# The same instructions at other addresses: SBUF tiles of the large matmuls moved to multiples of 2 KB

## The chip, the cores and the metric

The kernel runs on one core of a Trainium2 chip. The metric is the device time of one execution in microseconds (us); lower is better. SBUF is the on-chip memory, 128 partitions wide; in this text an address is a byte offset within a partition, and a tile of 1024 float32 columns takes 4,096 bytes of it. PSUM is the memory that TensorE writes its results to.

## The reference, cut to what matters

The reference runs a sequence of 256 positions of width 1024 through four layers and then through one further block, all in float32. Layers 0 and 3 use banded attention with 16 heads and a relative bias, layer 1 a gated linear attention, layer 2 a differential attention; each is followed by a layer norm, a SwiGLU feed-forward part of hidden width 2816 and a second layer norm. The last block is a SwiGLU part, a mixer (indexed sparse attention beside a gated short convolution), a cross-attention to 256 memory positions, and another SwiGLU part, with RMS norms between them.

```
h = layer_norm(DN_ALPHA * h + mixer_i(h), ln1_g[i], ln1_b[i])
h = layer_norm(DN_ALPHA * h + (silu(h @ Wg) * (h @ Wu)) @ Wd, ln2_g[i], ln2_b[i])      # i = 0..3
...
h = h + 0.5 * rms_norm(swiglu(rms_norm(h)))        # and the mixer, cross-attention, a second swiglu
```

Nearly all arithmetic is in the products of the 256 x 1024 activations with weight matrices: some 340 MB of weights are read once.

## The kernel before, in words

**Split products.** A float32 product is made out of three float32r products. Every weight piece of 128 x 1024 arrives by DMA in a tile `raw` (5 buffers); ScalarE writes its rounded part `wh` (L274, 10 buffers) and VectorE the rest `wl` (L275, 10 buffers). Activations are held transposed and split in the same way: `sth0`, `stl0`, `sth1`, `stl1` (128 x 8 x 128, one buffer each, for the two halves of the sequence) for products that go in from width 1024, and `gth0`, `gtl0`, `gth1`, `gtl1` (128 x 4 x 128, two buffers each) for products that go out to width 1024. The function `mm3` then issues three matmuls: the weights are the moving operand, 512 columns at a time, and a 128 x 128 slice of the activations is the stationary operand, loaded anew for each matmul.

```
for o, w in zip(outs, whs): nc.tensor.matmul(o, xh, w, start=first, stop=False)   # L286
for o, w in zip(outs, wls): nc.tensor.matmul(o, xh, w, start=False, stop=False)   # L288
for o, w in zip(outs, whs): nc.tensor.matmul(o, xl, w, start=False, stop=last)    # L290
```

`lin` uses `st` slices and one PSUM bank named `lin`; slice number kt goes from 0 to 7, and the three matmuls of one kt follow one another. `lin_out` uses `gt` slices and two banks named `acc`, alternating between the halves of the output. There are 5,040 matmuls of 512 columns in `lin` and 2,256 in `lin_out`, and 48 of 200 columns. One product is the other way round: for the gate of layer 1 (L705 to L707) the moving operand is a 128-column slice of `sth` or `stl`, and the stationary one has 16 columns.

**Other tiles.** `t2` (4 buffers of 128 x 512), `q2`, `v2`, `b4`, `p4`, `pt4`, `bc`, `k4` (4,128 bytes, 2 buffers) and `sm` (20 buffers of 64 bytes) hold what lies between: keys, queries, probabilities, biases, gains, row sums. `ident` is the identity for transposes on TensorE (L332, L606); `mhalf` and `ones` are small constants.

**Order of work.** The two halves of the sequence are two generators that are stepped in turn, so that each weight piece serves both. The whole list of instructions is then put into an order for each engine by a planner (`plan_order`, `play`, `order_issue`): it simulates engines, buffers and DMA with fixed costs and due times, and its order is written into the program as dependences. The planner looks at each tile's name, at the region of the tile that an instruction touches, at the tag and at the number of buffers; it does not look at addresses.

**Addresses.** A pool gives each tag its buffers side by side, in the order in which tags are first asked for. In the compiled kernel before, four constants of the framework lie ahead of the pool, which begins at 16,512. The offsets from a multiple of 2,048 are: 128 for `h0`, `h1`, `raw`, `wh`, `wl` and `ident`; 704 for `sth0`, `stl0`, `t2`, `sth1`, `stl1`; 704 and 736 for `k4`; 768 for `q2`, `b4`, `p4`; 0 for `pt4`, `v2`, `gth0`, `gtl0`, `gth1`, `gtl1` and `bc`, which come right after `sm`.

Of the kernel before, what the change touches and what calls it, by code (L numbers as in the profile page):

```python
# [208 lines left out]
class Net:  # L209
# [154 lines left out]
    def setup(self):  # L364
        nc, A = self.nc, self.A
        self.cache = {}
        self.toep = {}
        self.h = [self.t(f"h{tt}", [128, D], 1) for tt in range(2)]
        for c in range(2):
            nc.sync.dma_start(self.h[0][:, 512 * c:512 * c + 512], A["x"][0, 0:128, 512 * c:512 * c + 512])  # L370
            self.emit_splits(1 + c)
        self.ident = self.t("ident", [128, 128], 1)
        make_identity(nc, self.ident)
        self.mhalf = self.t("mhalf", [128, 8], 1)
        nc.gpsimd.memset(self.mhalf, -0.5)
        self.ones = self.t("ones", [128, 1], 1)
        nc.gpsimd.memset(self.ones, 1.0)

    def setup1(self):
# [1046 lines left out]
```

## Time and profile before

| | |
|---|---|
| median of 3 runs | 1947.97 us (1946.9 to 1948.11) |
| the profiled execution | 1947.88 us, of which the span from first to last instruction is 1946.1 us |
| TensorE matmuls | 1918.8 us busy, 99% of the span |
| VectorE, ScalarE, GpSimd | 60%, 48%, 2% |
| mean granted clock of TensorE | 0.998 |
| DMA | 345.59 MB, mean 178 GB/s |

Matmuls overlap one another, and their ends are modelled, so the sum of their durations is more than the span; the pace is read from their starts. PE is TensorE's matmul, PEld its load of the stationary operand.

### The profile page before, as it was taken

How to read it: one execution, taken by the hardware profiler on the slowest of the kernel's cores; microseconds unless marked ns; L12 is line 12 of the kernel's file. 1: busy time of each engine (PE TensorE's matmuls, PEld its weight loads, DVE VectorE, ACT ScalarE, POOL GpSimd, SP SyncE). 2: the span in 40 equal slices, each digit the busy share in tenths (PEclk: the TensorE clock that was granted, in tenths of full speed). 3: DMA queues.
4: the chain of work that ended last, by engine and by line, in shares of the span. 5: the costliest groups of instructions: out<-in, count | busy, mean ns of one | idle time of the engine just before them, and what ended most of it. 6: DMA issues, size and time to landing. Idle time of an engine off the chain costs nothing.

```text
span 1946.1 us, 23881 instructions
## 1 busy us (share of the span) xinstructions
PE 1918.8 (99%) x8998; PEld 1535.1 (79%) x8998; DVE 1168.2 (60%) x1687; ACT 926.6 (48%) x1332; POOL 48.5 (2%) x71
## 2 busy tenths in 40 slices
PE   8999999999999999999999999999999999999998
PEld 6888887777888777888778888878887788788886
DVE  5565547666456767555756645664567957565454
ACT  5545444544444554444554544444444545545442
POOL 0000000000000000000000000000001000000000
PEclk9999999999999999999999999999999999999999
DMA  9536555646555545555544655465555456536562
GB/s 300 166 133 224 183 183 158 210 150 226 181 183 168 175 149 176 189 184 179 186 149 148 217 182 183 153 222 183 185 169 171 139 176 205 162 121 205 180 187 66
DMA packets 103293, 345.59 MB, mean 178 GB/s; under 512 B 13369, under 2 KB 20473, under 8 KB 103178
## 3 DMA queue, kind: packets, MB, share of 16 engines
q1 hardware_dynamic: 103178, 344.07, 54.3%
q8 instruction: 70, 1.15, 0.2%
q14 instruction: 45, 0.37, 0.1%
HBM read 341.01 MB, written 3.01 MB: 177 GB/s over the span
## 4 chain that ended last, share of the span: by engine, by line
PE 94%; DVE 3%; DMA 2%; ACT 1%; issue 0%; POOL 0%; SPq 0%; DVEq 0%; POOLq 0%; ACTq 0%
PE lin L286 20%; PE lin L288 19%; PE lin L290 19%; PE acc L288 9%; PE acc L286 9%; PE acc L290 9%; PE at L332 4%; PE lin L669 1%; PE at L581 1%; PE at L606 1%; DVE wl L275 1%; DMA raw<-in_weights_dram 1%; DMA toep<-t 1%; PE lin L965 0%; PE at L953 0%
## 5 line engine op out<-in xcount | busy, mean ns | idle before, releaser
L275 DVE TENSOR_TENSOR wl<-raw,wh 128x1024 fp32r<-128x1024 f32 (+2 forms) x614 | 742.0, 1217 | 462.0 <-ACT wh L274 461.7
L274 ACT ACTIVATE wh<-raw 128x1024 fp32r<-128x1024 f32 (+2 forms) x614 | 644.6, 1053 | 662.0 <-PE lin L290 423.4
L286 PE MATMUL lin<-wh,sth 128*128 128x512 f32 x1696 | 678.4, 404 | 5.0 <-DVE t L680 1.8
L288 PE MATMUL lin<-wl,sth 128*128 128x512 f32 x1696 | 670.1, 399 | 0.9 <-DVE wl L275 0.9
L290 PE MATMUL lin<-wh,stl 128*128 128x512 f32 x1696 | 670.6, 400 | 0.0
L286 PEld LDWEIGHTS lin<-wh,sth 128*128 128x128 f32 x1696 | 319.6, 189 | 82.2 <-issue 4.4
L290 PEld LDWEIGHTS lin<-wh,stl 128*128 128x128 f32 x1696 | 319.3, 188 | 75.8 <-issue 2.7
L288 PEld LDWEIGHTS lin<-wl,sth 128*128 128x128 f32 x1696 | 319.5, 188 | 72.3 <-DVE wl L275 2.0
L288 PE MATMUL acc<-wl,gth 128*128 128x512 f32 x752 | 252.3, 402 | 2.1 <-DVE wl L275 2.1
L286 PE MATMUL acc<-wh,gth 128*128 128x512 f32 x752 | 249.0, 400 | 0.7 <-ACT gth L337 0.7
L290 PE MATMUL acc<-wh,gtl 128*128 128x512 f32 x752 | 247.9, 398 | 0.0
L288 PEld LDWEIGHTS acc<-wl,gth 128*128 128x128 f32 x752 | 141.3, 189 | 34.8 <-DVE wl L275 3.0
L290 PEld LDWEIGHTS acc<-wh,gtl 128*128 128x128 f32 x752 | 141.7, 189 | 32.6 <-DVE gtl L883 0.3
L286 PEld LDWEIGHTS acc<-wh,gth 128*128 128x128 f32 x752 | 139.9, 188 | 32.5 <-issue 1.6
L332 PE MATMUL at<-ident,t 128*128 128x128 f32 x604 | 101.6, 274 | 4.0 <-DVE t L540 1.5
L332 PEld LDWEIGHTS at<-ident,t 128*128 128x128 f32 x604 | 75.5, 140 | 28.2 <-issue 3.1
L337 ACT ACTIVATE gth<-at 128x512 fp32r<-128x512 f32 (+1 forms) x98 | 55.4, 565 | 69.2 <-PE at L332 69.0
L561 DVE TENSOR_TENSOR t<-t,lin 128x512 f32<-128x512 f32 x60 | 41.2, 687 | 76.1 <-PE lin L290 76.1
L353 POOL TENSOR_TENSOR sm<-sm,mhalf 128x1 f32<-128x1 f32 (+2 forms) x42 | 36.7, 874 | 1651.9 <-DVE sm L480 939.9
L338 DVE TENSOR_TENSOR gtl<-at,gth 128x512 fp32r<-128x512 f32 (+1 forms) x98 | 64.1, 654 | 21.4 <-ACT gth L337 18.3
L592 ACT ACTIVATE p<-p,sm 128x128 f32<-128x128 f32 (+1 forms) x112 | 49.6, 444 | 42.7 <-DVE sm L590 42.6
L558 ACT ACTIVATE t<-lin 128x512 f32<-128x512 f32 x60 | 35.9, 598 | 50.2 <-PE lin L290 49.7
(158 smaller groups left out, 872.3 us busy)
## 6 DMA issues: line engine op xcount, KB each, us to landing
raw<-in_weights_dram SPq DMA_DIRECT2D x607, 512.0 KB, 3.5
b<-toep SPq DMA_DIRECT2D x40, 128.0 KB, 4.5
bc<-in_ln_g_dram SPq DMA_DIRECT2D x8, 512.0 KB, 4.4
bc<-in_ln_b_dram SPq DMA_DIRECT2D x8, 512.0 KB, 6.3
toep<-t SPq DMA_DIRECT2D x2, 768.0 KB, 10.1
bc<-in_ffn_post_g_dram SPq DMA_DIRECT2D x2, 512.0 KB, 3.5
p<-in_mem_dram SPq DMA_DIRECT2D x2, 512.0 KB, 6.3
out_dram<-h SPq DMA_DIRECT2D x4, 256.0 KB, 2.0
```

Source lines behind the costliest of these rows:

```text
L274: nc.scalar.activation(hi[:, c], src[:, c], AF.Copy)
L275: nc.vector.tensor_sub(lo[:, c], src[:, c], hi[:, c].bitcast(F32))
L286: nc.tensor.matmul(o, xh, w, start=first, stop=False)
L288: nc.tensor.matmul(o, xh, w, start=False, stop=False)
L290: nc.tensor.matmul(o, xl, w, start=False, stop=last)
L332: self.nc.tensor.transpose(b[:, k], src[:, k * 128:(k + 1) * 128], self.ident)
L337: self.nc.scalar.activation(hi, b[:, :n], AF.Copy)
L338: self.nc.vector.tensor_sub(lo, b[:, :n], hi.bitcast(F32))
L353: nc.gpsimd.tensor_tensor(out, x, self.mhalf[:, :x.shape[1]], op=OP.pow)
L558: nc.scalar.activation(gate[j], acc, AF.Silu)
L561: nc.vector.tensor_mul(s, s, acc)
L592: nc.scalar.activation(P[:, hh, :nk], P[:, hh, :nk], AF.Exp, bias=nm[:, hh:hh + 1], accum_out=sm[:, hh:hh + 1])
```

## The change

The change asks for tiles in another order at the start of `setup` and merges two small constants. `ident` (512 bytes), the 20 buffers of `sm` (1,280 bytes) and a tile `small` (128 bytes, which holds `mhalf` and `ones`) come first; then all buffers of the `gt` tiles and of `q2`, `v2`, `t2`, `b4`, `p4`, `pt4` and `bc`, each of a size that is a multiple of 2 KB; then `h0` and `h1`, `raw`, `wh`, `wl`, and, asked for where they were before, the `st` tiles. `k4` and the other odd sizes come behind them. Tiles asked for in `setup` only to fix the order are written and read by no instruction. The instructions that `setup` issues, and their order, are those of before.

```diff
+        self.ident = self.t("ident", [128, 128], 1)
+        self.sm(1)
+        small = self.t("small", [128, 32], 1)
+        self.mhalf, self.ones = small[:, :8], small[:, 8:9]
+        for tt in range(2):
+            self.new_gt(tt)
+        for tag, bufs in (("q2", 2), ("v2", 4), ("t2", 4)):
+            self.t(tag, [128, 512], bufs)
+        for tag in ("b4", "p4", "pt4", "bc"):
+            self.t(tag, [128, 1024], 2)
         self.h = [self.t(f"h{tt}", [128, D], 1) for tt in range(2)]
         for c in range(2):
             nc.sync.dma_start(self.h[0][:, 512 * c:512 * c + 512], A["x"][0, 0:128, 512 * c:512 * c + 512])
             self.emit_splits(1 + c)
-        self.ident = self.t("ident", [128, 128], 1)
         make_identity(nc, self.ident)
-        self.mhalf = self.t("mhalf", [128, 8], 1)
         nc.gpsimd.memset(self.mhalf, -0.5)
-        self.ones = self.t("ones", [128, 1], 1)
         nc.gpsimd.memset(self.ones, 1.0)
```

## Rows read from the trace of the kernel before

**Rows 1.** The page: engines with busy time and share, and the granted clock.

```profile
PE 1918.8 (99%) x8998; PEld 1535.1 (79%) x8998; DVE 1168.2 (60%) x1687; ACT 926.6 (48%) x1332; POOL 48.5 (2%) x71
...
PEclk9999999999999999999999999999999999999999
```

**Rows 2.** The chain that ended last, by engine and line.

```profile
PE 94%; DVE 3%; DMA 2%; ACT 1%; issue 0%; POOL 0%; SPq 0%; DVEq 0%; POOLq 0%; ACTq 0%
```

**Rows 3.** Timeline of PE, a run of lin: start, duration, line, operands, count.

```profile
273.08 0.39 PE L286 MATMUL lin<-wh,sth 128*128 128x512 f32 x1
273.31 0.39 PE L288 MATMUL lin<-wl,sth 128*128 128x512 f32 x1
273.54 0.39 PE L290 MATMUL lin<-wh,stl 128*128 128x512 f32 x1
273.78 0.39 PE L286 MATMUL lin<-wh,sth 128*128 128x512 f32 x1
...
285.44 0.40 PE L290 MATMUL lin<-wh,stl 128*128 128x512 f32 x1
```

**Rows 4.** Two such runs, windows: length, busy (count) by engine, clock, DMA.

```profile
273.08:285.44 12.36, 12.36 (x54) 9.91 (x53) 5.60 (x5) 5.80 (x6) 0.00 (x0) 1.00 0.57 178
579.23:591.60 12.37, 12.37 (x55) 9.91 (x54) 5.60 (x5) 5.81 (x6) 0.00 (x0) 1.00 0.57 178
```

**Rows 5.** Timeline of PE, a run of acc (lin_out).

```profile
1437.96 0.63 PE L288 MATMUL acc<-wl,gth 128*128 128x512 f32 x2
...
1444.47 0.62 PE L286 MATMUL acc<-wh,gth 128*128 128x512 f32 x2
```

**Rows 6.** Timeline of PE, a run in which lin and acc alternate.

```profile
612.28 0.39 PE L286 MATMUL lin<-wh,sth 128*128 128x512 f32 x1
612.51 0.39 PE L286 MATMUL acc<-wh,gth 128*128 128x512 f32 x1
...
614.35 0.39 PE L286 MATMUL acc<-wh,gth 128*128 128x512 f32 x1
```

**Rows 7.** Timeline of PE, layer 1's gate: 128 moving columns, 16 stationary.

```profile
320.26 0.22 PE L706 MATMUL lin<-stl,wh 128*16 128x128 f32 x1
...
320.50 0.22 PE L707 MATMUL lin<-sth,wl 128*16 128x128 f32 x1
320.56 0.22 PE L705 MATMUL lin<-sth,wh 128*16 128x128 f32 x1
320.62 0.23 PE L706 MATMUL lin<-stl,wh 128*16 128x128 f32 x1
320.68 0.22 PE L707 MATMUL lin<-sth,wl 128*16 128x128 f32 x1
320.74 0.22 PE L705 MATMUL lin<-sth,wh 128*16 128x128 f32 x1
...
321.58 0.22 PE L707 MATMUL lin<-sth,wl 128*16 128x128 f32 x1
```

**Rows 8.** Groups by form: count, busy us, mean ns, idle time ahead.

```profile
L286 PEld LDWEIGHTS lin<-wh,sth 128*128 128x128 f32 x1696 | 319.6, 189 | 82.2 <-issue 4.4 <-ACT sth L337 2.9 <-DVE t L680 2.5
L286 PEld LDWEIGHTS acc<-wh,gth 128*128 128x128 f32 x752 | 139.9, 188 | 32.5 <-issue 1.6 <-ACT gth L337 0.9
...
L338 DVE TENSOR_TENSOR gtl<-at,gth 128x512 fp32r<-128x512 f32 x86 | 59.1, 687 | 20.0 <-ACT gth L337 17.1
L337 ACT ACTIVATE gth<-at 128x512 fp32r<-128x512 f32 x86 | 50.8, 590 | 62.3 <-PE at L332 62.2
...
L338 DVE TENSOR_TENSOR stl<-at,sth 128x512 fp32r<-128x512 f32 x52 | 35.2, 688 | 16.9 <-ACT sth L337 16.7
...
L337 ACT ACTIVATE sth<-at 128x512 fp32r<-128x512 f32 x52 | 30.8, 597 | 39.9 <-PE at L332 39.2
```

**Rows 9.** What PE waited for: us in total, times, longest.

```profile
PE at L332 <- DMA h<-in_x_dram: 5.1, 2, 3.8
PE acc L288 <- DVE wl L275: 2.1, 2, 1.7
```

**Rows 10.** The chain in order of time, its first piece: start, length.

```profile
2.11 5.62 DMA h<-in_x_dram
```

## The prediction, as it was put on record before the result

> **What bounds the kernel now.** The page first: TensorE's matmuls are busy 99% of the span of 1946.1 us, no other engine over 60%, and the clock row shows full speed in every slice, which is the 2.4 GHz level [rows 1]. The chain that ended last is TensorE for 94% [rows 2], and what TensorE waited for by name is small: 5.1 us for the first piece of the input, 2.1 us and less for anything else [rows 9]. So the time is the pace of the matmuls, above all of the 7,296 with 512 columns, and only what changes that pace, or makes TensorE wait, is worth anything.
>
> The pace is read from starts, since ends are modelled. A run of `lin` goes from 273.08 to 285.44 us in 53 steps [rows 3]: 12.36 / 53 = 233.2 ns. Two such runs far apart take the same time within 0.01 us, beside 5.6 us of VectorE and 5.8 us of ScalarE work each [rows 4]; nothing in them varies with the weight buffer in use, and the ten buffers lie at ten addresses. 7,296 x 0.233 = 1,700 us, seven eighths of the span. One column for each cycle of 2.4 GHz would be 512 / 2.4 = 213.3 ns, so every such matmul carries about 20 ns over its columns. The question is whether part of these 20 ns comes from where operands lie.
>
> **The change part by part.** *Order of instructions.* `setup` issues the same DMAs, splits, identity and two constants in the same order. The tiles added have no instruction, and the planner reads names, regions and buffer counts, not addresses, so it should write the same order for every engine. Cost 0, the span of before and the 1.8 us around it staying as they are; an unused first buffer only turns a tag's rotation by one place.
>
> *Addresses.* The pool begins 128 bytes past a multiple of 2 KB; 512 + 1,280 + 128 = 1,920 bytes come first, so all that follows begins at 18,432 = 9 x 2,048, and stays on multiples of 2 KB through the `st` tiles. So the change does what it says, for three kinds of operand: the `gt` tiles were there already (offset 0), `wh` and `wl` go from 128 to 0, the `st` tiles from 704 to 0.
>
> *Stationary operand, 704 to 0.* The trace of before holds both cases. A load from `sth` takes 189 ns, one from `gth` 188 ns, of which a step of 233 ns hides all [rows 8]. Within `st`, slice kt begins at 704 + 512 kt, so slices 2 and 6 run over a multiple of 2,048 and the others don't; yet each group of three in the run starts 0.70 us after the one before, 273.08 to 273.78 and so on to 285.44 [rows 3]. So a load that crosses costs nothing that shows. What differs is the pace of `acc`: from 1437.96 to 1444.47 us lie 28 steps, 6.51 / 28 = 232.5 ns [rows 5], 0.7 ns under `lin`. If the offset of the stationary tile is the reason, `lin` gains 0.7 ns at the 4,414 places where one `lin` matmul follows another (counted in the trace's order, as the other counts of neighbours below): 3.1 us. If the two alternating banks or the repeated slice are, it gains nothing. Bounds 0 and 3.1 us; I take 0, because slices at 704, 1,216, 1,728 and 192 of 2,048 all give the same 0.70 us.
>
> *Moving operand, 128 to 0.* No 512-column matmul of before has its weights anywhere else, so this is bounded. A weight slice of 2,048 bytes at offset 128 crosses one multiple of 2 KB in each matmul; after the change none does. The nearest rows are the 128-column products of layer 1, where the moving operand is `st`: 22 steps from 320.26 to 321.58 us, 60.0 ns each [rows 7]. From 128 to 512 columns the step grows by 173.2 ns in 384 columns, 0.451 ns a column, which leaves 60.0 - 128 x 0.451 = 2.3 ns that does not grow with columns. What a start off the boundary costs once for each matmul is in those 2.3 ns: at most 2.3 x 7,296 = 16.8 us. And there slice 2 (the three rows at 320.56, 320.62 and 320.68) and slice 6 cross a multiple of 2 KB and the others don't, but the steps are 0.06 us through and through [rows 7]. With starts shown to 0.01 us and three steps in a row, a crossing costs 0 to some 3 ns, 0 to 22 us over all; I take 0, as no step stands out.
>
> *Other engines.* ScalarE writes `gth` in 590 ns and `sth` in 597, VectorE 687 and 688 [rows 8]: at most 7 ns for 52 calls, 0.4 us, under a TensorE that is busy. If that cover were gone it would still be 0.4 us. The loads of weights write to another offset; they are waited for nowhere in [rows 9], so a slower load has the depth of five `raw` buffers before it shows.
>
> *Start.* The first piece of the input, rows of 2 KB into `h0`, is on the path with 5.62 us [rows 10]; it now lands at offset 0 in place of 128. I take 0, with bounds of half a microsecond either way as an estimate, a tenth of that row. The Trainium skill, in DMA: Bandwidth & Descriptors, How a descriptor splits into AXI transactions, says that transfers are cut at multiples of 256 bytes. By it a 2 KB row at offset 128 makes nine transactions and an aligned one eight, which would make the start some 0.6 us shorter (5.62 / 9, an estimate) and the total 1947.3 us; no row here shows a transaction.
>
> **Sum.** 0 for the order, 0 for the stationary, 0 for the moving operand, 0 for the rest: the profiled execution's own 1947.88 us, with the median of the runs at 1947.97. I predict 1947.9 us. About 0.2%, 3.9 us, is what a measurement of this kernel can tell from no change.
>
> **The rivals.** *`lin` takes the pace of `acc`*: 1947.9 - 3.1 = 1944.8 us. For it: the 0.7 ns between [rows 3] and [rows 5], and 0 is the offset that `gt` has. Against: no dependence on kt.
>
> *The fixed part goes, or most steps take the best pace seen.* Where `lin` and `acc` alternate, nine steps from 612.28 to 614.35 us make 2.07 us, 230.0 ns each [rows 6], the lowest pace in the trace, and there moving and stationary operands of different offsets meet. If offsets set the pace and the new ones are good, the 4,414 and 1,787 steps of like kind gain 3.2 and 2.5 ns: 14.1 + 4.5 = 18.6 us, 1929 us; the fixed 2.3 ns gives about the same, 1931 us. For it: the pace does vary by 3 ns with the kind of neighbour. Against: the 230.0 ns came with unlike offsets, and the change makes all alike.
>
> *The 20 ns are the crossing itself.* 20 ns less the 2.3 is 17.6 ns, for 7,296 matmuls 128 us: 1819 us. The arithmetic fits, since a quarter of the 128-column slices cross too. But then the steps in [rows 7] would be 0.056 us for six slices and 0.073 for slices 2 and 6, and they are all 0.06. In TensorE: Matmul & The Clock Gate, Back-to-back issue gap, the Trainium skill gives N / 2.4 + 2.5 ns, which for 512 columns is 216 ns; the trace has 233.2 [rows 3], so by that page 17 ns of each step would be there to regain, some 1,822 us.
>
> *Alike offsets collide: slower.* After the change every moving slice and every stationary slice that is loaded under it begin at the same place of a 512-byte grid, slices 0 and 4 at the same place of 2 KB, in `lin` and `acc` alike. The only case for it is that neighbours with unlike offsets run at 230.0 ns and those with like ones at 233.2 and 232.5 [rows 3, 5, 6]. If only the 670 mixed neighbours lose their 3.2 ns, it is 2.1 us, 1950.0 us, too little to tell. If likeness of moving and stationary offset costs another such step, the 6,201 like neighbours lose 3.2 ns each: 19.8 us, 1967.7 us. It decides from 0.6 ns a step on, where it passes 3.9 us. Against it: in `acc` moving and stationary tiles are 128 apart and in `lin` 576, and neither is much the better.
>
> **How the numbers follow.** No pace changes: 0.53, 1947.9 us. `lin` takes the pace of `acc`: 0.14, of which I give a quarter to more than 3.9 us. Gains of 4 to 22 us: 0.12. The crossing: 0.04. Mixed neighbours alone lose: 0.05. A collision over 3.9 us: 0.12. So faster 0.04 + 0.12 + 0.04 = 0.20, same 0.53 + 0.10 + 0.05 = 0.68, slower 0.12. The range leaves out the crossing and about half of the larger gains below, and half of the collisions above, under 0.2 in all: 1937 to 1956 us. The likeliest case's own range is 1944 to 1951.8.
>
> **What would show it.** Right: a run of `lin` of 53 steps still takes 12.36 us, the run of `acc` 6.51 us for 28 steps, the alternating run 2.07 us for nine; loads of `sth` still 189 ns; the same counts of instructions on each engine; waits of PE as in [rows 9]. A `lin` run of 12.32 us would be the first rival, of 12.2 us or less the second, of 11.4 us the third, and more than 12.4 us the fourth. I am wrong if the start of a full-rate float32r read has a cost that neither the slices of `st` nor the 128-column products bring out, or if the new places of the buffers make the framework wait where it did not before; the second would show as PE waiting, with the paces as they were.

## The result and the profile after

The changed kernel takes 1916.47 us (1912.8 to 1916.84, 4 runs) where the one before took 1947.61 in the same session: 31 us faster; the ratio of the means is 0.9836, its 95% interval 0.9819 to 0.9853. The prediction of 1947.9 us was wrong, and the time lies below its range of 1937 to 1956.

The page of the changed kernel, its engine row, and the shares of its chain by engine:

```profile
PE 1885.8 (98%) x8998; PEld 1533.6 (80%) x8998; DVE 1168.1 (61%) x1687; ACT 927.9 (48%) x1332; POOL 48.2 (3%) x71
...
PE 94%; DVE 3%; DMA 1%; ACT 1%; issue 0%; POOL 0%; SPq 0%; DVEq 0%; POOLq 0%; ACTq 0%
```

Every engine has the count of instructions that it had in [rows 1], and the chain is TensorE's for the same 94% [rows 2]. The span went from 1946.1 to 1914.7 us, by 31.4. Loads, VectorE and ScalarE are busy as long as before within 1.5 us; the matmuls are 33.0 us shorter. So no wait went and no work went: the pace changed. The timeline of PE, for the same 54 instructions of `lin` as in [rows 3] (the line numbers behind L365 are 9 higher in the changed file, those of `mm3` are the same):

```profile
272.13 0.39 PE L286 MATMUL lin<-wh,sth 128*128 128x512 f32 x1
...
284.14 0.39 PE L290 MATMUL lin<-wh,stl 128*128 128x512 f32 x1
...
605.40 0.39 PE L286 MATMUL lin<-wh,sth 128*128 128x512 f32 x1
...
607.44 0.39 PE L286 MATMUL acc<-wh,gth 128*128 128x512 f32 x1
...
1414.69 0.62 PE L288 MATMUL acc<-wl,gth 128*128 128x512 f32 x2
...
1421.09 0.61 PE L286 MATMUL acc<-wh,gth 128*128 128x512 f32 x2
```

A step is the time from one matmul's start to the next one's. From 272.13 to 284.14 us, 53 steps take 12.01 us, 226.6 ns each, where [rows 3] had 233.2. The nine mixed steps of [rows 6] take 2.04 us, 226.7 ns, in place of 230.0. The 28 steps of `acc` take 6.40 us, 228.6 ns on average, in place of 232.5 [rows 5]; why not 226.7 too is told with the experiments. At 2.4 GHz, 226.7 ns are 544 cycles, 32 more than there are columns; 233.3 ns, `lin` before, are 560. The products with a 16-column stationary operand, in contrast, did not move:

```profile
318.43 0.22 PE L715 MATMUL lin<-stl,wh 128*16 128x128 f32 x1
...
319.74 0.22 PE L716 MATMUL lin<-sth,wl 128*16 128x128 f32 x1
```

22 steps in 1.31 us, 59.5 ns, where [rows 7] had 1.32 us. Where the time came from, in the groups by form (count, busy us, mean ns, idle time ahead), first of the kernel before:

```profile
L286 PE MATMUL lin<-wh,sth 128*128 128x512 f32 x1680 | 674.0, 405 | 4.4 <-DVE t L680 1.8 <-ACT sth L337 1.0 <-ACT t L620 1.0
L290 PE MATMUL lin<-wh,stl 128*128 128x512 f32 x1680 | 666.6, 401 | 0.0
L288 PE MATMUL lin<-wl,sth 128*128 128x512 f32 x1680 | 665.9, 400 | 0.9 <-DVE wl L275 0.9
L288 PE MATMUL acc<-wl,gth 128*128 128x512 f32 x752 | 252.3, 402 | 2.1 <-DVE wl L275 2.1
L286 PE MATMUL acc<-wh,gth 128*128 128x512 f32 x752 | 249.0, 400 | 0.7 <-ACT gth L337 0.7
L290 PE MATMUL acc<-wh,gtl 128*128 128x512 f32 x752 | 247.9, 398 | 0.0
```

and of the changed kernel, with two of its loads:

```profile
L286 PE MATMUL lin<-wh,sth 128*128 128x512 f32 x1680 | 666.9, 401 | 4.3 <-DVE t L689 1.8 <-ACT t L629 1.0 <-ACT sth L337 0.9
L290 PE MATMUL lin<-wh,stl 128*128 128x512 f32 x1680 | 660.2, 397 | 0.0
L288 PE MATMUL lin<-wl,sth 128*128 128x512 f32 x1680 | 658.8, 396 | 1.1 <-DVE wl L275 1.1
L288 PE MATMUL acc<-wl,gth 128*128 128x512 f32 x752 | 248.2, 396 | 2.3 <-DVE wl L275 2.3
L286 PE MATMUL acc<-wh,gth 128*128 128x512 f32 x752 | 246.4, 396 | 0.7 <-ACT gth L337 0.7
L290 PE MATMUL acc<-wh,gtl 128*128 128x512 f32 x752 | 244.6, 394 | 0.0
...
L286 PEld LDWEIGHTS lin<-wh,sth 128*128 128x128 f32 x1696 | 319.6, 189 | 74.6 <-issue 4.2 <-ACT sth L337 2.7 <-DVE t L689 2.6
L286 PEld LDWEIGHTS acc<-wh,gth 128*128 128x128 f32 x752 | 139.6, 188 | 30.1 <-issue 1.6 <-ACT gth L337 0.9
```

The three `lin` groups go from 2006.5 to 1985.9 us, 20.6 less, the three `acc` groups from 749.2 to 739.2, 10.0 less: 30.6 us, beside the 31.4 of the span. Those are modelled durations; by the starts, the 6,819 steps in which one of these products follows another are 31.9 us shorter in sum. The loads stay at 189 and 188 ns [rows 8]. What PE waited for stayed too, with the rows that answer to [rows 9]:

```profile
PE at L332 <- DMA h<-in_x_dram: 5.2, 2, 3.7
...
PE acc L288 <- DVE wl L275: 2.3, 2, 1.7
```

### The profile page after: what moved, and what is told of

Its sections match the earlier page's. It is cut to its first block, busy times and chain, and to the rows that moved or that the text cites. A ratio compares the mean times of both kernels' runs of the same rounds, so it can differ in the third digit from the quotient of the medians.

```text
span 1914.7 us, 23881 instructions
## 1 busy us (share of the span) xinstructions
PE 1885.8 (98%) x8998; PEld 1533.6 (80%) x8998; DVE 1168.1 (61%) x1687; ACT 927.9 (48%) x1332; POOL 48.2 (3%) x71
## 4 chain that ended last, share of the span: by engine, by line
PE 94%; DVE 3%; DMA 1%; ACT 1%; issue 0%; POOL 0%; SPq 0%; DVEq 0%; POOLq 0%; ACTq 0%
PE lin L286 20%; PE lin L288 19%; PE lin L290 19%; PE acc L286 9%; PE acc L288 9%; PE acc L290 9%; PE at L332 4%; PE lin L678 1%; PE at L590 1%; PE at L615 1%; DVE wl L275 1%; DMA toep<-t 1%; PE lin L974 0%; PE at L962 0%; DMA b<-toep 0%
## 5 line engine op out<-in xcount | busy, mean ns | idle before, releaser
L286 PE MATMUL lin<-wh,sth 128*128 128x512 f32 x1696 | 671.3, 400 | 4.9 <-DVE t L689 1.8
L288 PE MATMUL lin<-wl,sth 128*128 128x512 f32 x1696 | 663.0, 395 | 1.1 <-DVE wl L275 1.1
L288 PE MATMUL acc<-wl,gth 128*128 128x512 f32 x752 | 248.2, 396 | 2.3 <-DVE wl L275 2.3
L353 POOL TENSOR_TENSOR sm<-sm,small 128x1 f32<-128x1 f32 (+2 forms) x42 | 36.3, 864 | 1620.2 <-DVE sm L489 921.5
```

The source lines that it names most:

```text
L353: nc.gpsimd.tensor_tensor(out, x, self.mhalf[:, :x.shape[1]], op=OP.pow)
```

## The experiments

Three theories. **M**: a moving slice of 2 KB that crosses a multiple of 2 KB costs time. **S**: the offset of the stationary tile does. **D**: neither by itself, but the difference between the stationary and the moving offset. Of the kernel before, `lin` had moving 128 and stationary 704, `acc` 128 and 0; after the change all are 0, so the result alone fits all three. The table holds all kernels of the whole computation, with offsets of moving, `st` and `gt` tiles from a multiple of 2,048 bytes, the differences stationary less moving modulo 256, the step in the same 53 `lin` steps and 28 `acc` steps as above (from the windows below), and the time. The ratios are those to runs of the kernel before in the same session.

| kernel | moving, st, gt | lin, acc difference | lin, acc ns | us (runs), ratio to before |
|---|---|---|---|---|
| before | 128, 704, 0 | 64, 128 | 233.2, 232.5 | 1947.61 |
| after | 0, 0, 0 | 0, 0 | 226.6, 228.6 | 1916.47, 0.9836 [0.9819, 0.9853] |
| e1 | 0, 704, 0 | 192, 0 | 228.9, 228.2 | 1925.98 (1920.9 to 1927.72), 0.9883 [0.9868, 0.9899] |
| e2 | 128, 0, 0 | 128, 128 | 233.4, 232.5 | 1947.43 (1943.93 to 1949.86), 0.9999 [0.9990, 1.0008] |
| e3 | 128, 128, 128 | 0, 0 | 226.6, 227.5 | 1916.68 (1914.85 to 1920.06), 0.9841 [0.9825, 0.9858] |
| e5 | 128, 896, 384 | 0, 0 | 226.6, 228.2 | 1917.14 (1916.12 to 1917.98), 0.9846 [0.9831, 0.9861] |
| e6 | 128, 896, 256 | 0, 128 | 226.8, 232.5 | 1927.51 (1927.1 to 1928.99), 0.9902 [0.9885, 0.9918] |
| e7 | 128, 736, 224 | 96, 96 | 234.3, 233.9 | 1956.88 (1955.08 to 1960.88), 1.0044 [1.0028, 1.0059] |

**One part of the change at a time: e1 and e2.** In the changed kernel, padding in front of the `st` tiles brings these back to 704 and leaves the rest; or padding brings the weights back to 128 and the `st` tiles again to 0.

```diff
+        self.t("pad", [128, 176], 1)                          # e1, ahead of make_identity: st at 704
...
+        self.t("pad", [128, 32], 1)                           # e2, ahead of h: h, raw, wh, wl at 128
+        self.t("cst", [128, 900], 1)                          # e2, ahead of make_identity
+        self.t("pad2", [128, 88], 1)                          #     st at 0 again
```

> The changed kernel with the four st tiles moved to offset 704 of 2,048, where they were before; wh, wl and gt stay at 0. Three theories for the 31 us. Theory M: the moving slice crosses a multiple of 2 KB in each matmul and pays about 6.7 ns for it; then only the moving offset counts, a run of lin stays at 226.7 ns a step and the time at 1916.5 us. Theory S: the stationary offset counts; lin goes back to 233.3 ns, acc stays at 226.7, and of the 31 us some 22 are lost again: about 1938 us. Theory D: what counts is the difference of the two offsets, 0 after the change; here lin has 704 and acc 0, so lin slows and acc does not, again about 1938 us.

> The changed kernel with raw, wh and wl moved to offset 128, as before; st and gt stay at 0. Theory M: every slice crosses again, lin and acc at 232.5 to 233.3 ns a step, 1946 us. Theory S: lin stays at 226.7 ns; acc, which had this pair of offsets before and ran at 232.5 ns, would have to stay slow for another reason: about 1925 us. Theory D: both have a difference of 128, as acc before: 232.5 ns, about 1944 us.

Windows over the `lin` run and the `acc` run (length, then busy time and count of PE, PEld, DVE, ACT, POOL, granted clock, DMA share and GB/s), of e1 and then of e2:

```profile
269.18:281.31 12.13, 12.13 (x54) 9.97 (x53) 5.60 (x5) 5.79 (x6) 0.00 (x0) 1.00 0.58 184
1417.24:1423.63 6.39, 6.39 (x30) 5.26 (x28) 5.67 (x10) 5.75 (x11) 1.95 (x2) 1.00 0.24 83
```

```profile
274.40:286.77 12.37, 12.37 (x55) 9.96 (x53) 5.58 (x5) 5.81 (x6) 0.00 (x0) 1.00 0.54 186
1436.73:1443.24 6.51, 6.51 (x30) 5.29 (x29) 5.80 (x10) 5.87 (x11) 1.95 (x2) 1.00 0.23 82
```

With the weights at 0 and `st` at 704, `lin` runs at 12.13 / 53 = 228.9 ns; with the weights at 128 and every stationary tile at 0, nothing at all is gained. S falls with e2. M fits e2, but not that `lin` loses 2.3 ns again in e1, where no moving slice crosses. D has the direction in both, but not the sizes: it had 1938 us for e1, which took 1926, and 1944 for e2, which took 1947. In e2 `lin` and `acc` have the same difference, 128, and run at 233.4 and 232.5 ns, so a difference does not always fix the pace to the nanosecond: by the starts, 60 of the 80 runs of `lin` of 18 steps and more take 233.5 there and 20 take 232.4, of `acc` 2 and 7.

**All shifted together: e3.** One constant tile is 128 bytes wider, which shifts every tile behind it by 128: each 2 KB moving slice crosses a multiple of 2 KB again, no large operand is aligned, and all differences are 0.

```diff
-        small = self.t("small", [128, 32], 1)
+        small = self.t("small", [128, 64], 1)
```

> The changed kernel with every tile behind the small ones shifted by 128 bytes: moving and stationary operands all at offset 128, their difference 0. Theory M: 233 ns a step, about 1947 us, since all moving slices cross a multiple of 2 KB. Theory S: about 1947 us too, since no stationary tile is at 0. Theory D: 226.7 ns and 1916.5 us, as in the changed kernel.

Its two windows:

```profile
272.11:284.12 12.01, 12.01 (x55) 9.96 (x53) 5.59 (x5) 5.78 (x6) 0.00 (x0) 1.00 0.56 189
1416.02:1422.39 6.37, 6.37 (x29) 5.26 (x28) 5.66 (x10) 5.73 (x12) 1.94 (x2) 1.00 0.26 84
```

It keeps the whole gain. M falls, and with it any mixture of M and S; D alone is left.

**TensorE by itself: m1.** A small kernel leaves the whole computation out: blocks of 48 products of 512 columns, one matmul after another on two banks, each block with its own offsets of moving and stationary slices; no other engine works.

```
for mv, st, n, step, cols in blocks():          # offsets in bytes; step of the stationary slice; its columns
    for i in range(48):
        ...                                     # m0, s0: from mv, st and step
        nc.tensor.matmul(banks[i % 2][:cols, :n], sta[:, s0:s0 + cols], mov[:, m0:m0 + n], start=True, stop=True)
```

> Leaves the whole computation out and runs only float32r matmuls on one engine: blocks of 48, each with its own offsets of the moving and the stationary slice, 512 columns unless said, after a warm-up. Theory M: 226.7 ns a step in each block with the moving offset 0 whatever the stationary one, 233.3 with every other moving offset. Theory S: the same with the roles exchanged. Theory D: 226.7 ns where the two are equal, 233.3 where not. If no block is slower than another, the cost needs the other engines or the DMA as a partner.

Windows of one block each, from its first start to the next block's, 48 steps; columns as above. In order, moving and stationary offset are (128, 704), (128, 0), (512, 0), (0, 32), (0, 192), then (0, 0) and (128, 0) with one and the same slice loaded each time, then (0, 0) and (128, 0) with a stationary slice of 16 columns:

```profile
21.02:32.22 11.20, 11.20 (x49) 9.02 (x48) 0.00 (x0) 0.00 (x0) 0.00 (x0) 1.00 0.01 1
76.46:87.61 11.15, 11.15 (x49) 9.04 (x48) 0.00 (x0) 0.00 (x0) 0.00 (x0) 1.00 0.01 1
98.54:109.42 10.88, 10.88 (x49) 9.01 (x48) 0.00 (x0) 0.00 (x0) 0.00 (x0) 1.00 0.00 0
142.07:153.26 11.19, 11.19 (x49) 9.02 (x48) 0.00 (x0) 0.00 (x0) 0.00 (x0) 1.00 0.00 0
175.62:186.62 11.00, 11.00 (x50) 9.02 (x49) 0.00 (x0) 0.00 (x0) 0.00 (x0) 1.00 0.00 0
295.69:306.57 10.88, 10.88 (x49) 9.01 (x48) 0.00 (x0) 0.00 (x0) 0.00 (x0) 1.00 0.00 0
306.57:317.76 11.19, 11.19 (x49) 9.01 (x48) 0.00 (x0) 0.00 (x0) 0.00 (x0) 1.00 0.01 1
...
328.97:340.09 11.12, 11.12 (x50) 4.57 (x48) 0.00 (x0) 0.00 (x0) 0.00 (x0) 1.00 0.00 0
340.09:351.21 11.12, 11.12 (x49) 4.66 (x48) 0.00 (x0) 0.00 (x0) 0.00 (x0) 1.00 0.01 1
```

With all other engines idle, the offsets of before still give 11.20 / 48 = 233.3 ns and 11.15 / 48 = 232.3 ns, and a difference that is a multiple of 256 gives 10.88 / 48 = 226.7 ns. 32 bytes give 233.1 ns, 192 give 229.2. Differences of 256, 512 and 1,024 in either direction, 1,536, and equal offsets at six places from 64 to 1,024 all came to 226.7. So the other party is no other engine and no DMA. The Trainium skill (TensorE: Matmul & The Clock Gate, Step-by-step: what each phase is for) says that the load and the moving operand have a read port of SBUF each, so that a load takes no read bandwidth from the running product; by that alone one would expect that the offsets do not matter, and these windows, 10.88 against 11.20 us with nothing else at work, show that they do. With one and the same slice loaded each time there are two paces again, 226.7 and 11.19 / 48 = 233.1 ns; at the difference of 128 that is 0.8 ns more than in the block with changing slices. But the load has to be of the full 128 columns: with 16, both offsets take 11.12 / 48 = 231.7 ns. Ahead of this kernel D had 226.7 ns for equal offsets alone; that a difference counts modulo 256 came out of it, and e5 to e7, which were set down after it, test that.

**Padding alone, in the old order: e5, e6 and e7.** These are the kernel before with two paddings and nothing else, ahead of the `st` tiles and of the `gt` tiles:

```diff
     def new_gt(self, tt):
+        if "gth0" not in self.bufs_of:
+            self.t("pad2", [128, 48], 1)          # e5 and e7: 48; e6: 16
...
         nc.gpsimd.memset(self.ones, 1.0)
+        self.t("pad", [128, 48], 1)               # e5 and e6: 48; e7: 8
```

> The kernel before in its old order of tiles, with 192 bytes of padding ahead of the st tiles and 192 bytes more ahead of the gt tiles. Moving operands stay at remainder 128 of 2,048, st comes to 896 and gt to 384: no large operand lies at a multiple of 2 KB and the moving slices still cross one, but stationary minus moving is a multiple of 256 bytes everywhere (768 and 256). Theory D (the difference modulo 256 bytes sets the pace): lin and acc both at 226.7 ns a step, the whole gain, 1916.5 us (1913 to 1920). Theory M (a moving slice that crosses a multiple of 2 KB is slow): nothing changes, lin about 233.3 and acc about 232.4 ns, 1948 us. Theory S (the stationary operand's own offset): no gain either, 1948 us or slower, since gt leaves the multiple of 2 KB.

> The kernel before with 192 bytes of padding ahead of the st tiles and 64 more ahead of the gt tiles: moving at remainder 128 of 2,048, st at 896 (difference 768, a multiple of 256), gt at 256 (difference 128 modulo 256, as before). Theory D: the lin steps go to 226.7 ns and the acc steps stay at 232.4; by the three lin rows of the profiles before and after, which differ by 2006.5 - 1985.9 = 20.6 us, 1927 us (1924 to 1931). Theories M and S: no step changes, 1948 us.

> The kernel before with 32 bytes of padding ahead of the st tiles and 192 more ahead of the gt tiles, so that both stand at a difference of 96 bytes (modulo 256) from the moving slices: moving 128, st 736, gt 224 of 2,048. In the finer grid a difference of 96 took 234.3 ns, more than lin's 233.3 (+0.9 ns on some 4,650 steps) and acc's 232.4 (+1.9 ns on some 2,140). Theory D: slower than before by 0.9 x 4.65 + 1.9 x 2.14 = 8 us, 1956 us (1952 to 1960). Theories M and S: no operand gains or loses a multiple of 2 KB but gt, and the kernel e2, whose gt differed as little, took 1947 us: 1948 us.

The two windows of e5, of e6 and of e7:

```profile
272.16:284.17 12.01, 12.01 (x54) 9.95 (x53) 5.59 (x5) 5.78 (x6) 0.00 (x0) 1.00 0.58 187
1415.21:1421.60 6.39, 6.39 (x29) 5.26 (x28) 5.67 (x10) 5.74 (x12) 1.94 (x2) 1.00 0.25 83
```

```profile
272.64:284.66 12.02, 12.02 (x54) 9.95 (x53) 5.59 (x5) 5.78 (x6) 0.00 (x0) 1.00 0.58 185
1422.77:1429.28 6.51, 6.51 (x30) 5.27 (x28) 5.80 (x10) 5.87 (x12) 1.94 (x2) 1.00 0.24 82
```

```profile
279.45:291.87 12.42, 12.42 (x55) 9.98 (x54) 5.59 (x5) 5.82 (x6) 0.00 (x0) 1.00 0.54 179
1449.16:1455.71 6.55, 6.55 (x29) 5.27 (x28) 5.83 (x10) 5.91 (x11) 1.95 (x2) 1.00 0.26 81
```

D gave 1916.5, 1927 and 1956 us ahead of the runs; they took 1917.1, 1927.5 and 1956.9. With 384 bytes of padding the old order of tiles has the whole gain in e5, and there no operand of the large products stands at a multiple of 2 KB. In e6 the `lin` run is down to 12.02 us and the `acc` run still takes the 6.51 us of [rows 5]. And e7 makes the same program slower than it was, by 9 us, with padding alone.

**Behind a transpose: m3.** In the changed kernel not every step is at 226.7 ns. The timeline of PE ahead of the `lin` run shown above:

```profile
268.92 0.60 PE L332 MATMUL at<-ident,t 128*128 128x128 f32 x4
269.27 0.48 PE L286 MATMUL lin<-wh,sth 128*128 128x512 f32 x1
269.59 0.40 PE L288 MATMUL lin<-wl,sth 128*128 128x512 f32 x1
...
271.68 0.62 PE L290 MATMUL acc<-wh,gtl 128*128 128x512 f32 x2
```

The first product behind the four transposes takes 0.32 us to the next; the nine steps from 269.59 to 271.68 take 2.09 us, 232 ns each, as slow as before the change; then the pace settles. The `acc` run begins right behind such transposes, hence its 228.6 ns. The small kernel m3, again without the computation, puts 1, 4 or 8 transposes ahead of runs of 24 products.

```
for k in range(n): nc.tensor.transpose(at[:, ...], raw[:, ...], ident)        # n = 4, 1, 8
for i in range(24): nc.tensor.matmul(...)                                      # as in m1
```

> TensorE alone, all other work left out: runs of 24 products behind 1, 4 or 8 transposes, at differences of 0, 704 modulo 256 (192), 576 (64) and -128. Theory D: at difference 0 the steps first wander between 224 and 236 ns, as in the changed kernel behind its transposes, and then hold 226.7 to the end of the run; at 64 they come to 233.3, at -128 to 232.3, at 192 to 229. Rival: what the steps take behind a transpose is set by other engines' work in the kernel, and on TensorE alone they hold their pace from the first or second step on.

The first run at difference 0, from its second start over nine steps and then over its last 13 steps:

```profile
22.43:24.52 2.09, 2.09 (x11) 1.69 (x10) 0.00 (x0) 0.00 (x0) 0.00 (x0) 1.00 0.03 8
24.52:27.46 2.94, 2.94 (x14) 2.44 (x13) 0.00 (x0) 0.00 (x0) 0.00 (x0) 1.00 0.00 0
```

That is 232 ns a step and then, within the rounding to 0.01 us, the 226.7. By the starts in its trace, all 54 runs at differences that are multiples of 256 wander like this for 3 to 11 steps, mostly 3, 6 or 10, and then hold 226.7 ns to the end of the run; the rival, that other engines unsettle the pace, falls. (At 128, 17 of 18 runs go through a pattern of seven steps, 232.4 ns on average, and one alternates between 237 and 229 ns, 233.5: one difference can have two paces.) So the gain is paid only after the 3 to 11 steps behind each transpose or change of work: in the changed kernel 4,661 of the 6,819 steps are inside a settled stretch (they and both neighbours within 225.5 and 228.5 ns, counted from starts), and in these lie 29.3 of the 31.9 us. That is why 6.6 ns a step (233.2 less 226.6) on 5,040 products of `lin` and 5.8 on 2,256 of `lin_out`, 33.3 + 13.1 = 46.4 us, did not come in full.

**Is there a better difference? m2 and m4.** m2 takes blocks as in m1 at finer differences; m4 takes runs as in m3 for all differences from 0 to 252 in steps of 4. Both leave the computation out.

```diff
-    b.append((0, st, 512, 512, 128))                     # m1: 16, 32, 64, 128, 192, ...
+    b.append((0, d, 512, 512, 128))                      # m2: 24 values from 4 to 252
...
+    return [(0, d, n) for n in (4, 1) for d in range(0, 256, 4)]          # m4, 3 runs of 24 each
```

> Steps of blocks of 48 products on TensorE alone, all other work left out, as in the first grid of offsets, now with differences between its points (4 to 252 bytes), other widths of the stationary operand and other numbers of moving columns. Theory D: no difference beats a multiple of 256 bytes (226.7 ns); those from 32 to 64 bytes stay near 233 and those from 128 to 192 fall from 232 to 229. If the pace goes by single words or by 16-byte or 64-byte groups, differences inside one group share a pace. A difference below 226.7 ns would give a faster layout than the changed kernel's.

> TensorE alone, all other work left out: runs of 24 products behind 4 and behind 1 transposes, for every difference of stationary and moving offset from 0 to 252 in steps of 4 bytes. In the finer grid 216 and 252 reached 226.7 ns from their first step, out of a block that had not; difference 0 needs 3 to 11 steps behind a transpose and makes a run of 24 in 5.31 to 5.35 us from first to last start. If theory D holds with 0 as the only settled point, none beats 0. If 216 or 252 settle at once behind transposes too, their runs take about 0.315 + 22 x 0.2267 = 5.30 us less the settling, near 5.30 us, some 0.05 us less than 0, and a kernel with that difference would gain up to 10 us more on the changed one; if they settle later or not, nothing beats 0.

In m2, 216 and 252 also came to 226.7 ns, 4 stayed at 232.3, 96 at 234.3, and nothing went below 226.7. The windows of m4, from first to last start of one run of 24 behind four transposes, at differences 0, 120, 132, 240, 216, 252 and 156:

```profile
22.84:28.16 5.32, 5.32 (x26) 4.41 (x25) 0.00 (x0) 0.00 (x0) 0.00 (x0) 1.00 0.01 3
564.52:569.82 5.30, 5.30 (x26) 4.40 (x25) 0.00 (x0) 0.00 (x0) 0.00 (x0) 1.00 0.00 0
618.31:623.69 5.38, 5.38 (x27) 4.42 (x25) 0.00 (x0) 0.00 (x0) 0.00 (x0) 1.00 0.00 0
1106.97:1112.31 5.34, 5.34 (x27) 4.41 (x26) 0.00 (x0) 0.00 (x0) 0.00 (x0) 1.00 0.00 0
998.84:1004.27 5.43, 5.43 (x27) 4.42 (x26) 0.00 (x0) 0.00 (x0) 0.00 (x0) 1.00 0.00 0
1160.94:1166.39 5.45, 5.45 (x27) 4.41 (x25) 0.00 (x0) 0.00 (x0) 0.00 (x0) 1.00 0.00 0
...
726.54:732.23 5.69, 5.69 (x27) 4.44 (x25) 0.00 (x0) 0.00 (x0) 0.00 (x0) 1.00 0.00 0
```

Behind transposes 216 settles in one run of six and 252 in none: the promise of m2 does not hold. Of the 64 differences only 120 is level with 0 (5.315 against 5.323 us on the mean of six runs, 0.35 ns a step). By the starts, 132 comes to 226.7 ns in all six runs, behind up to ten slower steps, and 240 in three of six, with means of 5.34 us for both; 156 is the worst at 5.69 us, 243 ns a step once past its start. Nothing points to a layout that beats the changed kernel by an amount that could be told, so none was run.

## Why the prediction was wrong, point by point

**Right:** the order of instructions, their counts, the waits, the loads and the other engines are as before; the start too, since the first piece of the input is on the path with 5.61 us where it had 5.62 [rows 10], so that the 0.6 us set beside the sum did not come. The only thing that moved the time was the pace of the 7,296 products. "What would show it" held as a test: `lin` at 12.01 us is under the 12.2 us that it gave as the mark of the second rival.

**The step that failed** is the one on the stationary operand: "I take 0, because slices at 704, 1,216, 1,728 and 192 of 2,048 all give the same 0.70 us". The observation is true and tests nothing. The slices lie 512 bytes apart, so all four have the same remainder modulo 256 and the same difference of 64 to the moving slice. Offsets were looked at operand by operand against 2 KB, and what counts is one against the other, with a period of 256 bytes (e3, e5, m1). Whether the 0.7 ns between `lin` and `acc` were their two differences, 64 and 128, stays open: m1 gives 233.3 and 232.3 ns for just these, but 128 has the paces 232.4 and 233.5, and in e2, with 128 in both, `lin` and `acc` are 0.9 ns apart in the windows all the same.

**The bound on the moving operand failed with it:** "what a start off the boundary costs once for each matmul is in those 2.3 ns". Those 2.3 ns came from products with a 16-column stationary operand, and with 16 columns the offset has no effect (231.7 ns either way in m1, 59.5 ns before and after in the gate). And 128 moving columns hide it as well: with full loads, m2 has 111.7 ns for them at differences 0 and 64 alike. The nearest row was of another kind than the thing to be bounded, and a line through two different kinds of product is no bound for either. Both bounds together, 16.8 and 3.1 us, come to 19.9 (25 with the 22 us allowed for a crossing in place of the 16.8), and the gain is 31.

**The rivals.** `lin` at the pace of `acc`: no, both went to a pace that the trace of before does not hold. Gains of 4 to 22 us: the nearest in time, and its remark that the pace does vary with offsets was right, but its price rested on the 230.0 ns of mixed neighbours, which also fell, to 226.7. The crossing: no, moving slices cross in every product of e3 and e5, which have the whole gain. The Trainium skill's 216 ns for 512 columns (TensorE: Matmul & The Clock Gate, Back-to-back issue gap), named beside that rival and given there as the gap of a matmul by itself, is not reached by these float32r products with a load each: at none of the 64 differences of m4 does the pace settle below 226 ns. The collision of alike offsets had the right variable, the difference, with the wrong sign: alike is the good case. That `acc` at a difference of 128 and `lin` at 576 ran nearly alike was held against it; two points out of a period of 256 bytes, neither of them at a multiple of it, are no evidence that the variable is idle. With chances of 0.20, 0.68 and 0.12 the weight lay on "nothing shows", for want of a pair of rows that differed in this and nothing else.

**Shown and open.** Shown: the pace of back-to-back products of 512 columns with 128-column loads depends on stationary less moving offset modulo 256, with every other engine idle, and padding chosen by it moved the whole kernel to 1917, 1927 and 1957 us as expected; the steps between these products are 31.9 us shorter, the span 31.4. Not shown is what happens inside: that the load's reads and the moving reads get in each other's way in SBUF is one reading, and it does not say why loads of 8 to 96 columns, which read less, run at 230 to 232 ns at both offsets tried. Open too are why 120 and 132 settle, and 240, 216 and 16 now and then; what chooses between the two paces of 128; and why the nine mixed steps were at 230.0 ns before.

## What to carry to other kernels

Where the span is back-to-back TensorE products of 512 columns with a fresh 128-column load each, take the offset of the stationary slice less that of the moving slice modulo 256 bytes as a parameter: 0 was as good as any, the others cost up to 16 ns of 227 a step, and some bytes of padding set it. For fewer columns it has to be tried again: m1 has 173.3 against 175.9 ns for 384 columns at differences 0 and 128, but 120.0 against 118.8 for 256, and m2 146.7 ns for 320 at both 0 and 64. Before a trace is taken as evidence that an address does not matter, see whether its cases differ in any remainder that could matter, and take a bound only from instructions of the same shape. Transposes strewn among the products cost more than themselves, since the 3 to 11 steps behind each run at about the old pace.

## What the runs showed of the hardware that was not expected

- The settled step is 544 cycles for 512 columns; at difference 0 m1 has 416 (173.3 ns) for 384 and 288 (120.0 ns) for 256, and m2 352 (146.7 ns) for 320: 32 cycles over the columns each time. It is no rule for every width: m2's 448, 480 and 504 columns take 202.5, 216.6 and 226.7 ns, 38 to 40 cycles over, the last as long as 512. 128 and 192 columns both take 111.7 ns.
- The pace at one difference can depend on what went before: 16 held 226.7 ns in m1 behind a block that had settled, and 233.4 ns in m2 behind one that had not; in m4 it settled in one run of six. At 128 it is one of two: in m4 the three runs behind four transposes take the pattern of 232.4 ns and the three behind one take that of 233.5.
- A smaller load does not help: with 8 to 96 stationary columns m2 shows 230 to 232 ns at differences 0 and 128 alike, with 120 columns 233.3, though a 16-column load is busy 4.57 / 48 = 95 ns and a full one 188.
